# Feed-forward operands and the ring of split weights moved to addresses 64 bytes past a multiple of 128

## The chip, the cores and the metric

One core of one Trainium2 chip runs the whole kernel. The metric is the device time of one execution in microseconds (us), from three runs. The profile is one further execution on the same core; its rows count from that execution's first instruction.

## What is computed

One layer of a hybrid decoder on 512 prompt rows and 64 sample rows (576 columns in the kernel, which keeps everything transposed), width 1024:

```python
x = x + 0.5 * swiglu(rmsnorm(x, p['ffn1_norm']), p['ffn1_w_gate'], p['ffn1_w_up'], p['ffn1_w_down'])
h = rmsnorm(x, p['mix_norm'])
proj = h @ p['w_in']
...
x = x + jnp.concatenate([y_lru, y_pool], axis=-1) @ p['w_out']
x = x + cross_attend(rmsnorm(x, p['xattn_norm']), mem_k, mem_v, p['xattn_wq'], p['xattn_wo'])
x = x + 0.5 * swiglu(rmsnorm(x, p['ffn2_norm']), p['ffn2_w_gate'], p['ffn2_w_up'], p['ffn2_w_down'])
```

`swiglu(x, g, u, d)` is `(silu(x @ g) * (x @ u)) @ d` with an inner width of 2816. The two feed-forward steps are the first and the last of these lines.

## The kernel before

**Arithmetic.** Every large matrix product runs in float32r, split in two: a value is the sum of a rounded part (`h`, high) and the remainder (`l`, low), and a product is three matmuls: high by high, high by low, low by high (`mm3`, L159; `product`, L323). The stationary operand (128x128 weights, loaded by the PEld rows of the trace) is a weight block; the moving operand (288 columns, half of the 576) is a norm's output, a gated activation, or another activation.

**Stages.** Step f1 (`ffn`, L331, called at L688) runs from 0 to about 402 us, then the mixer's projections (`in_l`, `in_p`, `in_g`, then `wo`), the cross attention (`k`, `q`, `ss`, `s`, `v`, `sv`, `o`, `xo`), and from about 739 us step f2 (the same `ffn`, called at L1177) with the final norm in its last group.

**A step.** Of 22 chunks of 128 inner columns the first 3 (f1) or 2 (f2) are done with plain products (`std`, L351: two matmuls in a row with the same weights, one for each half of the columns). Each later chunk is done with seven products of twelve matmuls (`product`), on combinations of halves that `prepare_a` and `prepare_b` (L400, L412) make from the raw weights. From the fifth chunk on, the down projection of the group of chunks before (`down`, L448, names `pd`, `hh`, `hl`, `dh`, `dl`) is interleaved between the products by `fill` (L564); it too runs two matmuls per weight block. What is left of it runs alone after the last chunk: all of the last group in f1 (`down` with `after`, L629), in f2 as the tail with 320 and then 256 columns (L655 on). The order of TensorE's matmuls is fixed by a chain of dependencies in `mm` (L130).

**Where the operands lie.** Each SBUF partition is a byte range in which pools stack up from the left, or down from the right end (`side="right"`). Tiles are rounded to 32 bytes. The pools that matter, with the offset of their matmul operands from a multiple of 128 bytes as the built program places them:

| pool, tiles | what | offset |
|---|---|---|
| `wp`: `wr`, `wh`, `wl` (L71, L150, L348, L396) | raw weights and the ring of split weights; the stationary operand of all projections, and of the products but one | 96 |
| `s1`: `n1h`, `n1l` (L284, L679) | f1's normed input, moving | 96 |
| `f1`: `hh`, `hl`, `dh`, `dl`, `oh`, `ol` (L417, L442, L479) | f1's gated activations (moving) and down weights, and the seventh product's weights (stationary) | 64 |
| `s2`: `n2h`, `n2l` (L1154) | f2's normed input, moving | 64 |
| `f2`: as `f1` (L1177) | the same for f2 | 96 |
| `tail`: `th`, `tl` (L444) | down weights of f2's last group | 64 |
| `r1`, `r2`: `nm`, `y`, `nx`, `q` (L180) | moving operands of the projections between the steps | 96 |
| `xa`: `mh`, `ml`, `kk`, `pp` | operands of the cross attention | 64 |

All strides inside these tiles are multiples of 128 bytes (288 columns are 1152 bytes, a weight block's row 512), so a tile's offset holds for each of its slices. Below, a pair such as 96/64 is the offset of the moving operand over that of the stationary one.

Of the kernel before, what the change touches and what calls it, by code (L numbers as in the profile page):

```python
# [9 lines left out]
F32 = mybir.dt.float32  # L10
# [6 lines left out]
P = 128  # L17
# [48 lines left out]
def hybrid_step(ctx, tc, a):  # L66
# [3 lines left out]
    const = ctx.enter_context(tc.tile_pool(name="const", bufs=1))  # L70
    wp = ctx.enter_context(tc.tile_pool(name="wp", bufs=WSB))  # L71
    rows = ctx.enter_context(tc.tile_pool(name="rows", bufs=2))


    now, ends = {}, {}

    def begin(name, **kw):
        cm = tc.tile_pool(name=name, reuse_waits="tile", **{"bufs": 1, **kw})
        now[name] = cm.__enter__()
        ends[name] = cm  # L80
        return now[name]

    def end(*names):
        for name in names:
            ends.pop(name).__exit__(None, None, None)
            now.pop(name)
# [16 lines left out]
        return cst[:, c:c + 1]  # L103

    x = const.tile([P, DC, T], F32, name="x")
    ones = const.tile([P, 1], F32, name="ones")
    v.memset(ones, 1.0 / (DC * P))
    ident = const.tile([P, P], F32, name="ident")
# [32 lines left out]
    def split(hi, lo, src, scale=None):  # L141

        if scale is None:
            s.copy(hi, src)  # L144
            v.tensor_tensor(out=lo, in0=src, in1=f(hi), op=ALU.subtract)  # L145
        else:
            s.activation(hi, src, AF.Copy, scale=scale)
            v.scalar_tensor_tensor(out=lo, in0=src, scalar=scale, in1=f(hi), op0=ALU.mult, op1=ALU.subtract)
# [68 lines left out]
    def row_factor(accs, name, ps, n=T, parts=2):  # L217

        offs = blocks(n, parts)
        k = len(offs)
        ps = ps[:, 512 - k:512]
        u, y, q = (rows.tile([P, 8], F32, tag=f"rf{i}", bufs=1, name=f"rf{i}_{name}")[:, :k] for i in range(3))
        for i, o in enumerate(offs):
            for j, part in enumerate(accs):
                mm(ps[:, i:i + 1], lhsT=part[:, o:o + P], rhs=ones, start=j == 0, stop=j == len(accs) - 1)
        v.tensor_scalar(u, ps, EPS, None, op0=ALU.add)
        rsqrt(q, u, y)
        return q  # L230
# [92 lines left out]
    def product(out, w, n, b, start):  # L323

        for k in range(KP):
            for i, (qw, qx) in enumerate(((0, 0), (0, 1), (1, 0))):
                mm(out, lhsT=w(qw, k), rhs=n.part(qx, k, b), start=start and k == 0 and i == 0,
                   stop=k == KP - 1 and i == 2, skip_group_check=True)


    def ffn(name, n, fp, turn, plain, head=False):  # L331
# [240 lines left out]
        def finish_chunk(c):  # L572
            w, U, g, h_, l_ = c
            product(U, w["22"], n, T4, False)
            v.tensor_mul(g[:, :HT], U, g[:, :HT])
            split(h_, l_, g)

        for f in range(plain, FFC):
# [44 lines left out]
            fill()  # L623
            before = w, U, g, hh[gi][:, f - g0, :], hl[gi][:, f - g0, :]
        finish_chunk(before)
        after = turn()
        if after:
            down(gi, after)
# [11 lines left out]
        def finish(c0, c1, q, cuts):  # L640
            n2, h = c1 - c0, (c1 - c0) // 2
            pr = dual("rs")
            for i, o in enumerate(blocks(n2)):
                mm(pr[:, o // h, o % h:o % h + P], lhsT=q[:, i:i + 1].to_broadcast([P, P]), rhs=ident,
                   start=True, stop=True)
            for j0, j1 in zip(cuts, cuts[1:]):
                y = x[:, j0:j1, c0:c1]
                for i in range(2):
                    yh = y[:, :, i * h:(i + 1) * h]
                    v.tensor_mul(yh, yh, pr[:, i, :h].unsqueeze(1).to_broadcast([P, j1 - j0, h]))  # L650
                nc.sync.dma_start(a["o_y"][:, j0:j1, c0:c1], y)
# [23 lines left out]
            before_ = [acc[:, c0:c1], sq]  # L675
        finish(c0, c1, row_factor(before_, "f1", pd, c1 - c0), (0, 4, 6, 8))


    n1 = HalfNorm("g1", "n1", begin("s1", side="right"), acc=False)  # L679

    def to_mixer():
        nonlocal nm
        end("s1")
        nm = Norm("gm", "nm", begin("r1", side="right"))
        return nm.add

    nm = None
    ffn("f1", n1, begin("f1"), to_mixer, STD[0], head=True)  # L688
    end("f1", "ff")


# [3 lines left out]
    if True:  # L695
# [213 lines left out]
        for c in range(LC):  # L909
            gate_out(c)  # L910
    nc.sync.dma_start(a["o_small"], small)
    end("mix")


# [258 lines left out]
    def to_tail():  # L1173
        end("s2")
        begin("tail")

    ffn("f2", n2, begin("f2", side="right"), to_tail, STD[1])  # L1177
    end("f2", "tail", "ff")

# [110 lines left out]
```

## Time and profile before

| | |
|---|---|
| median of 3 runs | 1149.78 us (1148.24 to 1150.13) |
| profiled execution, its own time | 1148.76 us |
| its span, first to last instruction | 1146.7 us |
| TensorE matmul (PE) busy | 1129.4 us, 98% |
| weight loads (PEld) busy, beside the matmuls | 1113.0 us, 97% |
| VectorE (DVE) busy | 835.0 us, 73% |
| ScalarE (ACT) busy | 544.0 us, 47% |
| granted TensorE clock, mean | 0.997 |

Successive matmuls overlap in the trace: a row's duration (some 290 ns for 288 columns) is the way through the array, and the next one starts after some 132 ns. What a matmul costs is therefore the distance between starts, here called its pitch. It is read from the start times of a timeline, or as a window's length over the number of matmuls in it (a window counts up to three that only reach into it).

### The profile page before, as it was taken

Reading aid. Unit: us, or ns where it says so; the run is one execution under the profiler, and the core shown is the slowest. Engines: PE = TensorE matmul, PEld = TensorE weight load, DVE = VectorE, ACT = ScalarE, POOL = GpSimd, SP = SyncE. Lnnn points to the kernel's source line nnn. Section 1 sums busy time; section 2 is a strip of 40 time slices with the busy share of each in tenths; the row PEclk is TensorE's granted clock in tenths of the full one; section 3 lists DMA queues with packets and bytes.
Section 4 is the critical chain, followed back from the end, with each engine's and each line's share of the span. In section 5 each row is a group of like instructions: output and inputs, shape, how many; then the busy total and the mean of one; then the engine's idle time right before and its main releaser. Section 6 shows DMA issues by size and latency. Waiting matters only on the chain.

```text
span 1146.7 us, 20764 instructions
## 1 busy us (share of the span) xinstructions
PE 1129.4 (98%) x8634; PEld 1113.0 (97%) x8634; DVE 835.0 (73%) x1335; ACT 544.0 (47%) x852; POOL 24.1 (2%) x47
## 2 busy tenths in 40 slices
PE   8999999999999999999999999999999999999996
PEld 8999999999999999999998879999999999999996
DVE  8887787788774788977634566769877877877664
ACT  8644344444432555875622564545443443443343
POOL 0000000000000022110000000000000000000000
PEclk9999999999999999999999999999999999999998
DMA  8223233233221352232655753212333332332212
GB/s 294 94 83 110 75 93 101 83 95 115 80 81 51 116 177 60 71 128 87 224 199 181 281 201 93 74 37 84 93 93 91 94 92 75 106 104 72 88 47 83
DMA packets 44285, 126.30 MB, mean 110 GB/s; under 512 B 4832, under 2 KB 9952, under 8 KB 44064
## 3 DMA queue, kind: packets, MB, share of 16 engines
q1 hardware_dynamic: 41808, 122.84, 34.4%
q10 hardware_dynamic: 2384, 2.15, 0.6%
q8 instruction: 67, 1.10, 0.4%
q14 instruction: 26, 0.21, 0.1%
HBM read 120.16 MB, written 4.81 MB: 109 GB/s over the span
## 4 chain that ended last, share of the span: by engine, by line
PE 94%; DVE 3%; ACT 1%; issue 1%; DMA 0%; DVEq 0%
PE pd L132 25%; PE pu L132 23%; PE pc L132 11%; PE pa L132 5%; PE q L132 5%; PE wo L132 5%; PE xo L132 4%; PE pg L132 3%; PE k L132 2%; PE v L1024 2%; PE in_l L132 2%; PE in_p L132 2%; PE o L132 1%; PE s L132 1%; PE puc L132 1%; PE ss L992 1%
## 5 line engine op out<-in xcount | busy, mean ns | idle before, releaser
L132 PE MATMUL pd<-hh,dl 128*128 128x288 f32 (+2 forms) x644 | 139.6, 295 | 0.0
L132 PE MATMUL pd<-hh,dh 128*128 128x288 f32 (+2 forms) x644 | 139.1, 295 | 0.0
L132 PE MATMUL pd<-hl,dh 128*128 128x288 f32 (+2 forms) x644 | 138.9, 294 | 0.0
L132 PEld LDWEIGHTS pd<-hh,dh 128*128 128x128 f32 x644 | 103.9, 188 | 0.0
L132 PEld LDWEIGHTS pd<-hh,dl 128*128 128x128 f32 x644 | 103.5, 188 | 0.1
L132 PEld LDWEIGHTS pd<-hl,dh 128*128 128x128 f32 x644 | 103.2, 188 | 0.0
L144 ACT CAST oh_b<-r 128x512 fp32r<-128x512 f32 x39 | 24.2, 621 | 119.6 <-PE pa L132 107.1
L144 ACT CAST wh_e<-r 128x1024 fp32r<-128x1024 f32 x39 | 41.0, 1052 | 63.0 <-PE pu L132 56.9
L144 ACT CAST dh<-wr_d 128x512 fp32r<-128x512 f32 (+1 forms) x74 | 48.7, 658 | 40.8 <-PE pd L132 29.9
L464 DVE TENSOR_TENSOR x<-pd,x 128x576 f32<-128x576 f32 x72 | 54.3, 754 | 18.1 <-PE pd L132 18.1
L145 DVE TENSOR_TENSOR wl_e<-r,wh_e 128x1024 fp32r<-128x1024 f32 x39 | 47.7, 1223 | 13.2 <-ACT wh_e L144 13.2
L144 ACT CAST wh_g<-r 128x1024 fp32r<-128x1024 f32 x39 | 41.1, 1055 | 33.0 <-DVE r L420 29.2
L145 DVE TENSOR_TENSOR dl<-wr_d,dh 128x512 fp32r<-128x512 f32 (+1 forms) x74 | 54.0, 730 | 0.0
L145 DVE TENSOR_TENSOR wl_g<-r,wh_g 128x1024 fp32r<-128x1024 f32 x39 | 47.7, 1224 | 7.3 <-ACT wh_g L144 5.4
L145 DVE TENSOR_TENSOR wl_a<-r,wh_a 128x1024 fp32r<-128x1024 f32 x39 | 47.6, 1220 | 3.4 <-ACT wh_a L144 3.0
L603 DVE TENSOR_TENSOR g<-pc,u 128x288 f32<-128x288 f32 x39 | 17.8, 457 | 40.9 <-PE pc L132 40.6
L132 PE MATMUL pu<-n2h,wl_a 128*128 128x288 f32 x160 | 47.4, 296 | 0.0
L132 PE MATMUL pu<-n2h,wh_a 128*128 128x288 f32 x160 | 47.4, 296 | 0.0
L132 PE MATMUL pu<-n2l,wh_a 128*128 128x288 f32 x160 | 46.8, 293 | 0.5 <-DVE n2l L145 0.5
L610 DVE TENSOR_TENSOR g<-pa,rstd_n 128x288 f32<-128x288 f32 x39 | 17.8, 457 | 39.8 <-PE pa L132 39.4
L144 ACT CAST wh_a<-r 128x1024 fp32r<-128x1024 f32 x39 | 40.9, 1050 | 8.8 <-PE xo L132 3.5
L132 PE MATMUL pu<-n1l,wh_a 128*128 128x288 f32 x152 | 44.8, 295 | 0.0
(496 smaller groups left out, 3682.0 us busy)
## 6 DMA issues: line engine op xcount, KB each, us to landing
r<-f_gu SPq DMA_DIRECT2D x78, 512.0 KB, 3.7
wr_d<-f_d SPq DMA_DIRECT2D x48, 256.0 KB, 2.8
wr_d<-f_d SPq DMA_DIRECT2D x32, 320.0 KB, 3.1
ck<-ck SPq DMA_DIRECT2D x16, 512.0 KB, 4.6
cv<-cv SPq DMA_DIRECT2D x16, 512.0 KB, 7.1
wr_i<-w_in SPq DMA_DIRECT2D x12, 512.0 KB, 3.7
wr_s<-f_s SPq DMA_DIRECT2D x8, 512.0 KB, 4.6
wr_o<-w_out SPq DMA_DIRECT2D x8, 512.0 KB, 3.6
```

What stands on the lines that cost most here:

```text
L132: i = te.matmul(*args, **kw)
L144: s.copy(hi, src)
L145: v.tensor_tensor(out=lo, in0=src, in1=f(hi), op=ALU.subtract)
L464: v.tensor_add(halves(x[:, j, :]), pd[j][:, :, :HT], halves(x[:, j, :]))
L603: v.tensor_add(g[:, HT:], C, u2)
L610: v.tensor_mul(g[:, :HT], A, r[:, :HT])
L992: te.matmul(sps[b * 32:(b + 1) * 32, g, :ML], lhsT=z[:, 4 * g + b, j, :], rhs=t[:, b, :], start=j == 0, stop=j == DC - 1)
L1024: te.matmul(ps[:, m, :HD], lhsT=lhs[:, kd, ms], rhs=w[wi][:, k, :], start=kd == 0 and i == 0, stop=kd == DC - 1 and i == 2)
```

## The change

An unused tile of 8n float32, that is 32n bytes, is allocated in four pools. It shifts what follows it. The const pool lies at the left end, `wp` and `rows` behind it; `s1` and `f2` lie at the right end.

```diff
+    def odd(pool, n):
+
+        pool.tile([P, 8 * n], F32, bufs=1, name="odd")
...
     x = const.tile([P, DC, T], F32, name="x")
+    odd(const, 3)
     ones = const.tile([P, 1], F32, name="ones")
...
         finish_chunk(before)
+        if not head:
+            odd(fp, 1)
         after = turn()
...
         finish(c0, c1, row_factor(before_, "f1", pd, c1 - c0), (0, 4, 6, 8))
 
+    odd(rows, 1)
+
 
     n1 = HalfNorm("g1", "n1", begin("s1", side="right"), acc=False)
+    odd(now["s1"], 1)
```

(`fp` is the step's pool; `head` is true in f1 alone.) In the built program `wp` moves by 96 bytes, from offset 96 to 64; `n1h` and `n1l` from 96 to 64; all of `f2` from 96 to 64. What lay at 64 still does: `f1`'s and `s2`'s operands, the tail's and the attention's move by 128 or not at all. `r1` and `r2` stay at 96, since nothing is added in them. `ident` goes from 64 to 32, `ones` from 32 to 0. Every engine's instructions are the same as before in number, kind, shape, order and awaited semaphore counts; only addresses differ.

| matmuls of 288 columns | number | before | after |
|---|---|---|---|
| f1 plain products, and products from `wp` | 288 + 1368 | 96/96 | 64/64 |
| f1 products from `oh`, `ol` | 228 | 96/64 | 64/64 |
| f1 down projection | 1056 | 64/64 | 64/64 |
| f2 plain products, and products | 192 + 1680 | 64/96 | 64/64 |
| f2 down projection without the tail | 816 | 96/96 | 64/64 |
| `in`, `wo`, `q`, `xo` | 576 + 3 x 384 | 96/96 | 96/64 |

Of 256 columns, the 192 of `k` go from 64/96 to 64/64 and the 192 of `v` (weights moving) from 96/64 to 64/64; of the tail's 120 of 320 and 120 of 256 columns, 90 each go from 96/64 and 30 each from 96/96 to 64/64.

## Rows read from the trace of the kernel before

**Rows 1.** The page: busy time by engine, and the chain that ended last.
```profile
span 1146.7 us, 20764 instructions
...
PE 1129.4 (98%) x8634; PEld 1113.0 (97%) x8634; DVE 835.0 (73%) x1335; ACT 544.0 (47%) x852; POOL 24.1 (2%) x47
...
PE 94%; DVE 3%; ACT 1%; issue 1%; DMA 0%; DVEq 0%
```

**Rows 2.** Waits of PE alone: engine, line, releaser, us in total, times, longest.
```profile
PE pg L132 <- ACT wh L144: 5.5, 1, 5.5
PE rs L132 <- DVE rf_f L238: 1.4, 1, 1.4
PE pd L132 <- DVE x L661: 1.0, 2, 0.5
```

**Rows 3.** Timeline of PE: start, us, instruction; equal work of f1, first and last.
```profile
64.67 0.42 PE L132 MATMUL pd<-hh,dh 128*128 128x288 f32 x2
...
366.89 0.30 PE L132 MATMUL pu<-n1h,wl_a 128*128 128x288 f32 x1
```

**Rows 4.** The same view of f2, the same work.
```profile
795.34 0.42 PE L132 MATMUL pd<-hh,dh 128*128 128x288 f32 x2
...
1097.88 0.30 PE L132 MATMUL pu<-n2h,wl_a 128*128 128x288 f32 x1
```

**Rows 5.** Windows, tile pd alone: stretch, us, busy (count) by engine, clock, DMA.
```profile
64.60:366.80 302.20, 124.54 (x798) 111.58 (x798) 23.35 (x31) 0.00 (x0) 1.00 0.30 90
795.20:1097.70 302.50, 125.30 (x798) 112.26 (x798) 23.35 (x31) 0.00 (x0) 1.00 0.31 90
```

**Rows 6.** Windows, tile pa alone (product from `oh`, `ol`), the same stretches.
```profile
64.60:366.80 302.20, 31.61 (x216) 29.67 (x216) 8.24 (x18) 6.52 (x17) 1.00 0.30 90
795.20:1097.70 302.50, 31.42 (x216) 29.60 (x216) 8.24 (x18) 6.52 (x17) 1.00 0.31 90
```

**Rows 7.** Windows, PE: stretches of one kind of matmul without a stop.
```profile
368.00:400.00 32.00, 32.00 (x242) 1.00 0.33 95
495.00:525.00 30.00, 30.00 (x227) 1.00 0.42 135
705.00:735.00 30.00, 30.00 (x233) 1.00 0.29 88
743.00:751.00 8.00, 8.00 (x63) 1.00 0.01 2
```

**Rows 8.** Timeline of PE in f1's down projection alone, 64/64.
```profile
379.82 0.43 PE L132 MATMUL pd<-hh,dh 128*128 128x288 f32 x2
...
381.42 0.43 PE L132 MATMUL pd<-hh,dh 128*128 128x288 f32 x2
```

**Rows 9.** Timeline of PE in `wo`, 96/96.
```profile
495.88 0.43 PE L132 MATMUL wo<-yh,wl_o 128*128 128x288 f32 x2
...
496.69 0.42 PE L132 MATMUL wo<-yh,wl_o 128*128 128x288 f32 x2
```

**Rows 10.** Timeline of PE in `xo`, 96/96.
```profile
709.50 0.42 PE L132 MATMUL xo<-ql,wh_x 128*128 128x288 f32 x2
...
711.06 0.42 PE L132 MATMUL xo<-ql,wh_x 128*128 128x288 f32 x2
```

**Rows 11.** Timeline of PE in `k`, 256 columns, 64/96.
```profile
556.88 0.28 PE L132 MATMUL k<-mh,wh_k 128*128 128x256 f32 x1
...
557.60 0.28 PE L132 MATMUL k<-mh,wh_k 128*128 128x256 f32 x1
```

**Rows 12.** Timeline of PE in f2's tail, 256 columns, 96/64.
```profile
1125.18 0.28 PE L132 MATMUL pd<-hh,th 128*128 128x256 f32 x1
...
1126.23 0.28 PE L132 MATMUL pd<-hh,th 128*128 128x256 f32 x1
```

## The prediction, made before the changed kernel ran

> **What bounds the kernel now.** First the page: TensorE's matmuls are busy 98% of the span, and the chain that ended last lies 94% on PE [rows 1]. Then PE's waits: the longest is 5.5 us at the start, and the next two make 2.4 us together [rows 2]. There is no wait to win; the time is the sum of some 8,600 matmul pitches. What bounds the kernel is how closely matmuls follow each other, and an address can act there alone. VectorE (73%) and ScalarE (47%) [rows 1] could change their pace with an address too; it would be hidden under PE, which hardly ever waits for them.
>
> Then the pitch. At the granted clock of 1.00 [rows 7], its 2.4 GHz level, 288 columns would take 120.0 ns. The trace shows more. In f1's down projection alone, 12 matmuls take 381.42 - 379.82 = 1.60 us: 133.3 ns each [rows 8]. In `wo` 6 take 0.81 us, 135 ns at this resolution [rows 9]; over 30 us, 227 counted less the two that reach in from the side, 133.3 ns [rows 7]. In `xo` 12 take 1.56 us: 130.0 ns [rows 10]. So 10 to 13 ns lie on top of the columns, and they differ by place: 3.3 ns between `wo` and `xo`, which have the same shape, the same ring of weights and the same offsets, 96/96. Hence the offset alone doesn't set the pitch; there are patterns that TensorE falls into and keeps. At 256 columns, `k` (64/96) takes 0.72 us for 6, 120.0 ns [rows 11], the tail (96/64) 1.05 us for 9, 116.7 ns [rows 12]. That offsets play some part is likely; what part, these rows leave open.
>
> **A comparison that the trace holds.** f1 and f2 run the same 2286 matmuls from the first interleaved down projection to the last product: 798 of `pd` and 1488 of products. f1 takes 366.89 - 64.67 = 302.22 us [rows 3], f2 1097.88 - 795.34 = 302.54 us [rows 4]. In f1 the products are 96/96 (one in seven 96/64) and `pd` is 64/64; in f2 the products are 64/96 and `pd` is 96/96. The whole differs by 0.32 us, but its parts don't agree. `pd` at 64/64 is busy 124.54 us, at 96/96 125.30 us [rows 5]: 0.76 us / 798 = 0.95 ns less each. The products must then be 0.76 - 0.32 = 0.44 us cheaper in f2: 0.30 ns each in favour of 64/96. Of that the product from `oh` alone has (31.61 - 31.42) / 216 = 0.88 ns in favour of 64/96 against 96/64 [rows 6].
>
> **The change part by part.** It removes, adds and moves no instruction, no DMA and no wait; SP's and POOL's queues are the same. Only pitches can change.
>
> 1. f1's products, 96/96 to 64/64. No product stands at 64/64 before; the nearest row is `pd` at 64/64, interleaved with them, 0.95 ns cheaper than at 96/96 [rows 5]. 1368 x 0.95 = 1.30 us less, taken in full. Bounds: 3.3 ns less each if they fall into the pattern of `xo` [rows 10], 1 ns more if all of them run at 133.3 ns [rows 8] instead of the 132.2 ns that f1's loop has on average (302.22 / 2285, [rows 3]).
> 2. f1's 228 products from `oh`, 96/64 to 64/64: only the moving operand shifts. Half of the step, 0.1 us less; bounds as in 1.
> 3. f2's down projection, 96/96 to 64/64, 816 matmuls: 0.95 ns each, 0.78 us less. Before and after of this part both stand in the trace, so it is the surest.
> 4. f2's products, 64/96 to 64/64, 1680: they have 0.30 ns of the 0.95 already, so 0.65 ns each, 1.09 us less.
> 5. The plain products, 288 in f1 and 192 in f2, run by themselves. Alone, 64/64 has 133.3 ns [rows 8], 96/96 the same in `wo` [rows 7], and 64/96 some 131 to 133 (8.00 us over 60 or 61 of the 63 counted, the last line of [rows 7]): nothing.
> 6. The projections between the steps, 1728 matmuls, go from 96/96 to 96/64, by the ring alone. The two nearest rows contradict each other: in the loop 96/64 is dearer than 64/96 by 0.88 ns [rows 6], alone at 256 columns it is cheaper by 3.3 ns [rows 11, 12]. I take nothing. Upper end: `xo` loses its pattern, 231 matmuls in its 30 us of [rows 7], 3.3 ns each, 0.8 us more, and the others stay. Lower end: the other 1344 gain it, 4.4 us less.
> 7. `k`, `v` and the tail, between 116.7 and 120.0 ns a matmul on either side [rows 11, 12]: `k` may gain 192 x 3.3 ns = 0.6 us, the tail's 120 of 256 columns lose 0.4 us and its 120 of 320 as much, `v` lose 0.6 us. Between ends of either sign and of this size I take nothing.
>
> What hides the edits that I cost at nothing outside PE: casts and subtractions with other addresses, under PE's 98%; if one became slower, PE's waits would show it. Sum: 1.30 + 0.10 + 0.78 + 1.09 = 3.3 us less. Against the profiled execution's own 1148.76 us (span 1146.7 and 2.1 around it) that is 1145.5; that execution lies 1.0 us under the median of the runs, so against the median 1149.78 - 3.3 = **1146.5 us**, 0.29% less.
>
> **The rivals.**
>
> *Nothing changes* (1149.8 us). For it: alone, 64/64 and 96/96 both run at 133.3 ns [rows 7, 8]; the whole loop differs by 0.1% between two placements [rows 3, 4]. It may be that only the distance between the two operands counts, which is a multiple of 128 in both, and the 0.95 ns of `pd` come from its neighbours, the products. Against it: f2's products stand at a distance of 32 and change theirs to 0. The page "SBUF — State Buffer" of the Trainium skill, under Specifications, speaks for this rival: it gives cachelines of 16 bytes, of which 1152 contiguous bytes touch 72 from an offset of 64 as from 96. By that rule the term for `pd` would be zero, and so would the sum; the 0.76 us of rows 5 do not follow from it. "TensorE: Matmul & The Clock Gate", Part 2, adds that a weight load does not take read bandwidth from the running matmul, as it has a port of its own; no row here can show a port.
>
> *The projections fall into the pattern of `xo`* (1142.1 us). That pattern is in the trace, 130.0 ns over 30 us [rows 7]; with 96/64 the 256-column rows are at their quicker value too [rows 12]. The lower end of 6 comes on top of the forecast: 1146.5 - 4.4. Against it: every other stretch of 96/96 sits at 133.3.
>
> *The products lock at 133.3 ns* (slower, 1153.7 us). Alone, 64/64 runs at 133.3 ns over 32 us without a break [rows 7, 8], one of the dearest patterns of the trace. In the loops, products and `pd` now disturb each other with three different placements, and the average is 132.2. With one placement for everything the loops may settle in the pattern of f1's pure stretch: 3276 products x 0.95 ns = 3.1 us more, and `xo` loses 0.8. It decides from the point where the two loops' average, 132.3 ns now, passes 132.8: 2 x 2286 x 0.5 ns = 2.3 us more. Against it: f1's loop already has 64/64 `pd`, and there it is the cheaper one.
>
> That the change doesn't do what it says is excluded for the two steps by the built program's addresses; for the projections between them it is partly so, as `r1` and `r2` stay at 96.
>
> **How the numbers follow.** Forecast 0.45: own range 1145 to 1148.5. Nothing 0.21. The pattern of `xo` 0.16. Locked 0.18. About 0.2% (2.3 us) is what a measurement of this kernel can tell from no change, that is, under 1147.5 or over 1152.1. Of the forecast's case about 0.31 lies below, 0.14 within; the second is all within; the third all below; of the fourth 0.16 above and 0.02 within. Faster 0.47, same 0.37, slower 0.16. The range takes in the first two cases whole, half of the third and half of the fourth: 1142.5 to 1152.5.
>
> **What the changed profile would show.** Right: the same work of f1 takes 302.22 - 1.4 = about 300.8 us and that of f2 302.54 - 1.8 = 300.7 us, and f2's `pd` falls from 125.30 to about 124.5 us busy. `pd` of f1, unchanged in offset, keeps 124.5; if it moves by as much as the rest, neighbours and not offsets set the pitch. `wo` at 133.3 ns and `xo` at 130.0 keep theirs within 1 ns, or term 6 is wrong. Wrong as a whole: f1's loop at 302 or more, or a wait of PE over 1 us that isn't in rows 2.

## The result, and the profile after

The changed kernel takes 1153.12 us, the median of 8 runs (1151.30 to 1153.97), against 1149.74 us for the kernel before on the same chip. The ratio is 1.0027, with a 95% interval from 1.0018 to 1.0036: slower by 0.27%. The forecast was 1146.5 us, 0.29% faster, in a range up to 1152.5. Sign and range are both wrong. The profiled execution took 1153.97 us.

First the page of the kernel after, its span, PE and the chain's engines, beside [rows 1]:

```profile
span 1151.2 us, 20764 instructions
...
PE 1134.0 (99%) x8634; PEld 1117.7 (97%) x8634; DVE 834.6 (72%) x1335; ACT 543.1 (47%) x852; POOL 25.5 (2%) x47
...
PE 94%; DVE 3%; ACT 1%; issue 1%; DMA 0%; DVEq 0%
```

The span grew by 4.5 us and PE's busy time by 4.6, on as many instructions. Next PE's waits after, beside [rows 2] (engine and line, releaser, us in total, times, longest):

```profile
PE pg L137 <- ACT wh L149: 5.6, 1, 5.6
PE rs L137 <- DVE rf_f L243: 1.4, 1, 1.4
PE pd L137 <- DVE x L668: 1.0, 2, 0.5
```

No wait is new. As the prediction had it, only the pitch of matmuls can have moved. Then the equal work of the two loops, in the timeline of PE after (start, us, instruction), beside [rows 3, 4]:

```profile
64.92 0.43 PE L137 MATMUL pd<-hh,dh 128*128 128x288 f32 x2
...
368.56 0.30 PE L137 MATMUL pu<-n1h,wl_a 128*128 128x288 f32 x1
...
797.94 0.42 PE L137 MATMUL pd<-hh,dh 128*128 128x288 f32 x2
...
1100.71 0.29 PE L137 MATMUL pu<-n2h,wl_a 128*128 128x288 f32 x1
```

f1's loop takes 303.64 us where it took 302.22 (+1.42), f2's 302.77 where it took 302.54 (+0.23). Next the windows of `pd` alone after (stretch, us, busy and count of PE, PEld, DVE, ACT, clock, DMA share, GB/s), beside [rows 5]:

```profile
64.90:368.50 303.60, 125.65 (x798) 113.04 (x798) 23.37 (x31) 0.00 (x0) 1.00 0.31 90
797.00:1100.00 303.00, 124.74 (x798) 111.85 (x798) 23.34 (x31) 0.00 (x0) 1.00 0.31 90
```

`pd` of f2 fell from 125.30 to 124.74 us, as forecast. `pd` of f1, whose own offsets didn't change, rose from 124.54 to 125.65: the sign that the prediction had named for neighbours. Last the plain stretches, windows of PE after (stretch, us, busy and count, clock, DMA share, GB/s), beside [rows 7]:

```profile
368.00:400.00 32.00, 32.00 (x242) 1.00 0.31 89
495.00:525.00 30.00, 30.00 (x227) 1.00 0.41 135
705.00:735.00 30.00, 30.00 (x227) 1.00 0.31 95
```

f1's pure stretch and `wo` are as they were. `xo` went from 233 matmuls in 30 us to 227: from 130.0 to 133.3 ns each, +0.95 us over its stretch.

About 1.5 us of the span's 4.5 are not the change's. In the tail of this execution the granted clock fell to 0.50, the 1.2 GHz level, for some 3.4 us, in which 19 matmuls are counted instead of 32: 13 at some 117 ns are 1.5 us. Windows of PE after:

```profile
1124.00:1127.00 3.00, 2.48 (x22) 1.00 0.00 0
1127.70:1131.10 3.40, 3.40 (x19) 0.50 0.00 0
1131.20:1134.00 2.80, 2.80 (x26) 1.00 0.00 0
```

The same windows of the kernel before:

```profile
1124.00:1127.00 3.00, 3.00 (x27) 1.00 0.00 0
1127.70:1131.10 3.40, 3.40 (x32) 1.00 0.00 0
```

Shortly ahead of the fall PE had stood for 0.52 us and then run eight narrow matmuls for the final norm; so it does in the kernel before, whose clock stayed. Of the eleven profiles of the layer taken later, six show such a drop (3.4 us long, once 6.8) and five don't. A kernel that is faster than before (`d64`) is among the six, and the ring alone, as slow as the change, is among the five. So the drop doesn't go with the offsets.

### The profile page after: what moved, and what is told of

It reads as the page before. It is cut to its first block, busy times and chain, and to the rows that moved or that the text cites. A ratio compares the mean times of both kernels' runs of the same rounds, so it can differ in the third digit from the quotient of the medians.

```text
span 1151.2 us, 20764 instructions
## 1 busy us (share of the span) xinstructions
PE 1134.0 (99%) x8634; PEld 1117.7 (97%) x8634; DVE 834.6 (72%) x1335; ACT 543.1 (47%) x852; POOL 25.5 (2%) x47
## 4 chain that ended last, share of the span: by engine, by line
PE 94%; DVE 3%; ACT 1%; issue 1%; DMA 0%; DVEq 0%
PE pd L137 25%; PE pu L137 23%; PE pc L137 11%; PE pa L137 5%; PE q L137 5%; PE wo L137 4%; PE xo L137 4%; PE pg L137 3%; PE v L1034 2%; PE k L137 2%; PE in_l L137 2%; PE in_p L137 2%; PE o L137 1%; PE s L137 1%; PE puc L137 1%; PE ss L1002 1%
```

## The experiments

Below, the **distance** of a matmul is the offset of its stationary operand less that of its moving one, modulo 128 bytes: the table of the change lists 96/96 and 64/64 at distance 0, 64/96 at 32, 96/64 at 96. Pitches in the two tables of stages are means of the distances between starts, from the traces' start times, without the steps over 160 ns. Each ratio is against runs of the kernel before on the same chip (medians from 1149.62 to 1150.60 us), so a ratio, and not a time, is what compares one experiment with another.

**Two kernels that should change nothing.** `p256` adds an unused tile of 256 bytes, so every operand keeps its offset in 128; `w12` runs one warm-up matmul more.

```diff
+    const.tile([P, 64], F32, name="pad")
```
```diff
-WARM = 11
+WARM = 12
```

> The kernel before with one unused tile of 256 bytes in the const pool, so that everything in the left pools moves by 256 bytes and every operand keeps its offset from a multiple of 128 and of 256. If offsets set the pitch: 1149.7 us within 0.1%, the same stretches (f1's equal work 302.2 us, xo at 130.0 ns). If the pattern that TensorE falls into is a matter of chance that any change of the program draws anew: 1147 to 1154, with xo at 130.0 or 133.3 ns and f1's equal work between 302 and 304.

> The kernel before with 12 instead of 11 warm-up matmuls at the start, all addresses unchanged; the weights arrive later than the warm-up ends, so its work itself is hidden. If offsets set the pitch: 1149.7 us within 0.1% and xo at 130.0 ns. If the pattern depends on when the matmuls begin: 1147 to 1154, with xo or f1's loop changed by 1 us or more.

`p256`: 1150.24 us, ratio 1.0001 [0.9993, 1.0009]. `w12`: 1150.86, 1.0006 [0.9997, 1.0015]. f1's loop takes 302.35 us in both, as before, and `xo` 38.51 in both. The time of f1's loop is no matter of chance or of the exact address.

One stage did change in `p256`: `wo`, at the same offsets 96/96. Windows of PE, first of the kernel before, then of `p256`:

```profile
505.00:529.00 24.00, 24.00 (x182) 1.00 0.52 170
505.00:529.00 24.00, 24.00 (x187) 1.00 0.52 173
```

About a hundred matmuls into `wo` its pitch goes from 133.3 to 130.0 ns and stays there, which saves 0.6 us. `s1` below does the same; `w12`, `f2` and `rest`, with the same offsets in `wo`, don't. So one stage at one distance can run at either pitch.

**The ring alone.** The change without its pads in `s1` and `f2`.

```diff
     x = const.tile([P, DC, T], F32, name="x")
+    odd(const, 3)
...
+    odd(rows, 1)
```

> Only the ring of split weights moves to 64 (const and rows tiles of the change); n1 and all of f2 stay at 96. f1's products are then 96/64, f2's products 64/64, the projections 96/64, both down projections as before. If offsets set the pitch and the ring is what costs: xo at 133.3 ns (0.95 us more) and f1's equal work near 303.8 us, time near 1152. If n1's move to 64/64 costs in f1: f1's equal work stays at 302.2, time near 1150.7. If chance: no relation to the change's stretches.

1153.42 us, ratio 1.0029 [1.0020, 1.0039]: the whole slowdown. The loops in its timeline of PE:

```profile
64.79 0.43 PE L137 MATMUL pd<-hh,dh 128*128 128x288 f32 x2
...
367.91 0.30 PE L137 MATMUL pu<-n1h,wl_a 128*128 128x288 f32 x1
...
797.36 0.43 PE L137 MATMUL pd<-hh,dh 128*128 128x288 f32 x2
...
1100.77 0.29 PE L137 MATMUL pu<-n2h,wl_a 128*128 128x288 f32 x1
```

Both loops lose: 303.12 - 302.22 = +0.90 us and 303.41 - 302.54 = +0.87. `xo`, in the window of its 30 us, has the change's 133.3 ns:

```profile
706.00:736.00 30.00, 30.00 (x227) 1.00 0.30 88
```

**The other parts, alone and together.** `s1` moves n1's pool alone, `f2` the second step's pool alone, `rest` both, so it is the change with its ring undone (against the change):

```diff
     x = const.tile([P, DC, T], F32, name="x")
-    odd(const, 3)
...
-    odd(rows, 1)
```

> One part alone: only n1's pool is moved (n1 from 96 to 64), ring and f2's pool stay at 96. Step 1's products become 64/96, as step 2's were in the kernel before. Distance theory (the pitch goes by the stationary operand's offset less the moving one's, modulo 128; 32 is on the cheap side, 0 and 96 on the dear one): step 1's products fall from 132.51 to about 132.3 ns, that is 1488 x 0.2 = 0.3 us, pd unknown by up to 1 ns either way (0.8 us); stretches outside step 1, xo's 38.5 us among them, unchanged; time 1149.0, range 1148.2 to 1150.2, ratio 0.998 to 1.000. Rival, absolute offset (operands at 64 are cheap): only one operand of the products at 64, half of the forecast's term 1, about -0.65 us. Rival, the prediction's terms were right and only the ring's xo loss was missed: as the absolute one. No theory gives a slowdown; one would mean that pd's neighbours decide.

> One part alone: only the second step's pool is moved (its pd from 96/96 to 64/64, its oh to 64); products stay 64/96, the ring and n1 at 96. Distance theory: pd stays at distance 0, so step 2's loop changes only through pd's neighbours: within 0.5 us of 302.7 either way, time 1149.7 +- 0.6, ratio 0.9995 to 1.0005. Prediction's term 3 (64/64 is cheaper for pd): pd falls from 132.30 to 131.3 ns, -0.8 us, time 1149.0. Everything ahead of step 2 as before, xo's 38.5 us among them.

> The change without its ring: n1 and f2's pool are moved to 64, the ring of split weights stays at 96. Theory R (the ring alone makes the loss: it puts the loops' products at distances that their cycle pays for, and takes xo out of its 130.0 ns state): the two parts, each without effect alone, stay without effect together, 1149.9 +- 0.8, ratio 0.9993 to 1.0008, xo 38.5 us, step 1's loop 302.3 and step 2's 302.5. Rival, parts that only act together (n1 and f2 at 64 cost time whatever the ring): step 1's loop unchanged, since f2's pool stands behind it, so the rival would have to act in step 2's and reach 303 us.

1150.05 us, 1.0002 [0.9993, 1.0011]; 1150.48, 1.0005 [0.9996, 1.0014]; 1150.02, 0.9997 [0.9986, 1.0007]: nothing, alone or together. `s1` took f1's products from distance 0 to 32, and their pitch stayed (132.51 and 132.53 ns), where the distance theory wanted 0.2 ns less. `f2` took `pd` from 96/96 to 64/64 and got 0.06 ns of the prediction's 0.95 (132.30 to 132.24): inside its bursts the steps fell from 132.37 to 131.88 ns, but the step from a burst to the next product rose from 131.91 to 134.26 and took it back.

**Streams of matmuls by themselves.** `micro` computes no layer: it runs, for each of 16 pairs of offsets, 96 matmuls of 288 columns as pairs (two halves on the same weights), then 96 singles.

```diff
+    for rep in range(REPS):
+        for om, ow in PLACES[rep]:
...
+                            mm(pair[:, h, :HT], lhsT=w[:, ow + k * P:ow + k * P + P],
+                               rhs=x[:, om + k * T + h * HT:om + k * T + h * HT + HT],
```

> Nothing of the layer is computed: TensorE runs 96 matmuls of 288 columns in pairs with the same weights, then 96 singly, for each of 16 placements (moving and stationary operand at 0, 32, 64, 96 bytes past a multiple of 128), twice; the second time each placement begins after three fp32 matmuls of one column. No other engine works beside it. If offsets set the pitch: each placement has one pitch, the same in both passes, and 64/64 differs from 96/96 and 96/64 by 0.3 ns or more. If only the distance counts: 0/0, 32/32, 64/64 and 96/96 agree within 0.2 ns. If patterns are entered by chance: the same placement gives 130 in one pass and 133 in the other.

From its timeline of PE, the first matmul of five successive stretches and one further on: moving at 0, stationary at 64 (pairs, singles), stationary at 96 (pairs, singles); then 32/32 (pairs, and the first of its singles).

```profile
72.51 0.43 PE L94 MATMUL pair<-mh,wh 128*128 128x288 f32 x2
...
85.20 0.29 PE L94 MATMUL one<-mh,wh 128*128 128x288 f32 x1
...
97.90 0.43 PE L94 MATMUL pair<-mh,wh 128*128 128x288 f32 x2
...
110.70 0.29 PE L94 MATMUL one<-mh,wh 128*128 128x288 f32 x1
...
123.60 0.43 PE L94 MATMUL pair<-mh,wh 128*128 128x288 f32 x2
...
149.19 0.42 PE L94 MATMUL pair<-mh,wh 128*128 128x288 f32 x2
...
162.00 0.29 PE L94 MATMUL one<-mh,wh 128*128 128x288 f32 x1
```

At distance 64, 96 matmuls take 12.69 us (132.2 ns each) as pairs and 12.70 as singles; at 96, 12.80 (133.3) and 12.90 (134.4); at 32/32, 12.81 as pairs. Over all 16 places the steady pitch goes by the distance, whatever the offsets themselves: pairs 132.2 at 64 and 133.3 at 0, 32 and 96; singles 132.2 at 32 and 64, 133.3 at 0, and 133.3 or 134.4 at 96. These are streams of one kind of matmul, and no place gave 130.0 here.

**Where 130.0 comes from.** `micro2` repeats such stretches, 48 matmuls each, behind one matmul of 8 to 296 columns.

```diff
+        for n in SLIPS:
+            mm(stop[:, :n], lhsT=wh[:, :P], rhs=mh[:, :n], start=True, stop=True)
```

> Only streams of matmuls, no layer is computed. Moving operand at 96, stationary at 64 past, 96, 0 and 32 in turn with the distance 0, 32, 64 and 96; ahead of each stretch of 48 stands one matmul of another width (8 to 296 columns), which shifts the phase between the stream and its weight loads. Distance theory in its plain form: each stretch settles at the pitch of its distance (pairs 132.2 at 64, 133.3 else; singles 132.2 at 32 and 64, 133.3 at 0 and 96) whatever the slip. Theory of several steady states: some slips leave a stretch at 130.0 ns, as xo showed, and only at some distances (0 among them, 96 not, by what the runs so far show of xo). Chance: pitches that differ between equal slips with no order in distance.

Four of these short matmuls in its timeline, ahead of pairs at distance 0, 96/96:

```profile
45.42 0.18 PE L91 MATMUL stop<-mh,wh 128*128 128x48 f32 x1
...
51.78 0.19 PE L91 MATMUL stop<-mh,wh 128*128 128x64 f32 x1
...
58.27 0.21 PE L91 MATMUL stop<-mh,wh 128*128 128x96 f32 x1
...
64.78 0.22 PE L91 MATMUL stop<-mh,wh 128*128 128x128 f32 x1
```

With its short matmul the stretch takes 6.36 us behind 48 columns, 6.49 and 6.51 behind 64 and 96: at distance 0 a stream of pairs has two steady pitches, 130.0 and about 133.3 ns, and its start decides which. Behind 16 to 48 and 280 columns it was 130.0, behind the others not (the stretch behind 8 columns began before the clock had risen). At distances 32, 64 and 96, and for singles, none of the 13 starts led to 130.0. But singles at distance 96 (96/64) settled at 134.4 ns behind 200 and 280 columns and at 133.3 behind the rest, so the 134.4 of `micro` need not belong to its one place.

`slip` tries it in the kernel before, at its own offsets: one extra matmul of 32 columns, overwritten at once, ahead of each chunk of `in`, `q` and the first halves of `wo`, and once in f1's pure stretch.

```diff
+    def jolt(ps, w, xx, k):
+        mm(ps[:, 0, :32], lhsT=w[0][:, k, :], rhs=xx[0][:, k, :32], start=True, stop=True)
...
+        if slip:
+            jolt(ps, w, xx, order[0])
```

> The kernel before, all offsets unchanged, and one extra matmul of 32 columns (its result is overwritten) ahead of the first matmul of each chunk of in, wo (first halves) and q, and once ahead of step 1's pure stretch. Theory S (at distance 0 a stream of pairs has two steady states, 133.3 and 130.0 ns, and a short matmul ahead of it puts it into the second): the stretches behind a slip run at 130.0 until something interrupts them; step 1's pure stretch 34.40 to about 33.7 us, q -0.4, in -0.6, wo -0.3, each slip itself paid with 0.11 us; time 1148.0, range 1147.0 to 1149.3. Rival, xo's 130.0 has another cause than a state entered at its start (its data, its queue, the place in the program): all stretches stay at 133.3 and the 30 slips cost 1 to 3 us: 1151 to 1153.

1152.82 us, ratio 1.0021 [1.0012, 1.0030]: a miss. In the timeline some chunks do change over:

```profile
420.70 0.43 PE L132 MATMUL in_l<-nml,wh_i 128*128 128x288 f32 x2
...
423.37 0.43 PE L132 MATMUL in_l<-nmh,wl_i 128*128 128x288 f32 x2
...
424.01 0.42 PE L132 MATMUL in_p<-nml,wh_i 128*128 128x288 f32 x2
...
426.35 0.42 PE L132 MATMUL in_p<-nml,wh_i 128*128 128x288 f32 x2
```

20 matmuls ahead of a slip take 2.67 us (133.5 ns), 18 behind it 2.34 us (130.0). But most of `q` and f1's pure stretch stayed at 133.3, and `xo`, to which nothing was done, lost its 130.0:

```profile
705.00:735.00 30.00, 30.00 (x227) 1.00 0.32 95
```

So `xo`'s pattern hangs on how the stream comes in, as well as on the distance.

**The loops' cycle by itself.** `micro3` runs 12 products as singles and 6 `pd` as pairs in turn, for 64 sets of distances, then three sets behind slips.

```diff
+    for ow in OFF:
+        for ou in OFF:
+            for od in OFF:
+                cycles(0, ow, ou, od, 10)
```

> Only streams of matmuls, no layer is computed: the loops' cycle of 12 products and 6 pd, ten times over for each of the 64 sets of distances (moving operand of the products at 0; their weights, pd's moving operand and pd's weights each at 0, 32, 64, 96), then three sets (all at 64 as in the change; step 1's of before; all at distance 64) behind slips of 13 widths. Theory of cycles (the mean of a cycle is set by the distances within the products, within pd and across their borders): sums of a cycle order as the loops did: all at 64 apart 2378 ns, step 1 of before 2381, ring at 64 with n at 96 2388, all together at one offset 2385 to 2392 and more than one value for it, by the slip. Rival (the loops' pitches came from other traffic, not from the addresses): all sets within 2 ns of one another.

A cycle of 18 takes from 2373 to 2407 ns by the set, so addresses alone do spread it by 1.4%. But the order is not that of the loops: all operands at one offset is among the cheap ones here (2376 ns) and the dear one in the change, and one and the same set (all 64 apart) settles at 2373 or at 2380 by the slip ahead, and at 2393 with all offsets 32 further on. So where kinds of matmul alternate, the distances alone don't give the time, even without the layer. This stream doesn't stand for the loops.

**The ring at the other two offsets, and everything 64 apart.** `r32` and `r0` place the ring alone at 32 and at 0. `d64` places ring, down weights, `oh` and `th` at 32 and all moving operands at 96; `d64s` is `d64` with all of them 32 bytes further on, so that the ring stands at 64 as in the change. The core of `d64` (`r32` and `r0` are as the ring alone, with 2 and 2, or 1 and 3, in place of 3 and 1; `d64s` has 3 in the const pool and 3 in a pool ahead of `s1`):

```diff
     x = const.tile([P, DC, T], F32, name="x")
+    pad(const, 2)
...
+        pad(fp, 2)
...
+        if not head:
+            pad(fp, 2, "pad2")
...
+        pad(tp, 2)
...
+    pad(rows, 3)
```

> All operands placed so that moving and stationary stand 64 apart: ring at 32, n1, n2, r1, r2 and hh at 96, dh and oh at 32, tail's th at 32. Distance theory: the plain stretches fall from 133.3 to 132.2 ns (f1's pure 258 matmuls, in 687, part of wo 376, q 449: about 1770 x 1.1 = -1.9 us), xo, which stood at 130.0, rises to 132.2 (288 x 2.2 = +0.6 us) as does k's and v's mix by at most 0.2; the loops' products and pd stay near 132.2, -0.3 to -1.5 us for both together. Time about 1147.8, range 1146.5 to 1149.5, ratio 0.997 to 1.000. Absolute-offset theory (64 is the cheap place): nothing stands at 64 here, so no gain: 1149.8 or, with xo's pattern lost, 1150.7. If the plain stretches stay at 133.3, the distance theory falls outside the stream measurement.

> The ring of split weights alone, at 32 in place of 96; everything else as before. Distance theory (stationary less moving, modulo 128; products in the loops at 64 about 132.2 ns, at 32 132.3 to 132.5, at 0 132.5 to 132.9, at 96 133.1): step 1's products (96/32, distance 64) fall to 132.2 ns, step 2's (64/32, distance 96) rise to 133.1; the plain stretches (96/32, distance 64) fall to 132.2 and in, wo and q as they did with all at 64 apart (91.35, 49.9, 59.5 us); xo 39.1 us. Time: -0.5 + 1.1 - 1.0 + 0.6, about 1149.9, range 1148.8 to 1151. Rival (any move of the ring away from where it stood costs, by slots and not by distance): both loops slower, in, wo and q unchanged, 1152 or more.

> The ring alone, at 0. Distance theory: step 1's products (96/0, distance 32) 132.3 to 132.5 ns, step 2's (64/0, distance 64) 132.2, so neither loop is slower; plain stretches (96/0, distance 32) stay at 133.3; xo, away from distance 0, loses its 130.0 ns: 38.5 to about 39.4 us. Time +0.9 - 0.3, about 1150.3, range 1149.3 to 1151.2. Rival (slots, not distance): both loops slower as with the ring at 64, 1152 or more.

> All operands 64 apart as in the run d64, and every one of them 32 bytes further on: ring, dh, oh and th at 64, where the change has them, and n1, n2, r1, r2, hh and xa's at 0. Distance theory: nothing but the differences counts, so the stage times are those of d64 (step 1's loop 301.98, step 2's 302.12, in 91.35, q 59.5, xo 39.1 us) and the time is 1147.3 +- 0.8, ratio 0.997 to 0.9985. Rival, the ring's place at 64 is in itself the dear one (absolute offset): loops at 303 and the time at 1151 or more.

`d64` 1147.31 us, ratio 0.9977 [0.9969, 0.9986]; `r32` 1151.03, 1.0007 [0.9999, 1.0016]; `r0` 1150.31, 1.0004 [0.9995, 1.0012]; `d64s` 1147.76, 0.9976 [0.9967, 0.9984]. The page of `d64s`, and its windows of PE:

```profile
span 1146.5 us, 20764 instructions
```
```profile
368.00:400.00 32.00, 32.00 (x244) 1.00 0.35 98
495.00:525.00 30.00, 30.00 (x230) 1.00 0.41 135
705.00:735.00 30.00, 30.00 (x229) 1.00 0.27 83
```

Two matmuls more fit into f1's 32 us and three into `wo`'s 30; `xo`, at 229, has neither 130.0 nor 133.3. (The span holds a drop of the clock in the tail, as in the profile after.) With the ring at 64 as in the change, the kernel is the faster one. The place itself is innocent; what it is paired with decides. Stages, us (a loop up to the first matmul behind it, `xo`'s last 288 matmuls with eight of f2 behind them, `q` with the score matmuls among it), and the pitch of `pd` in the loops, ns; below it the products. The distance there is that of six products of seven, those from the ring; the seventh, from `oh`, has the same only in `after`, `d64`, `d64s`, before's f2 and ring's f1:

| | before | ring | r32 | r0 | after | d64 | d64s |
|---|---|---|---|---|---|---|---|
| f1 loop | 302.35 | 303.25 | 302.63 | 302.42 | 303.77 | 301.98 | 302.10 |
| f2 loop | 302.67 | 303.54 | 303.75 | 302.81 | 302.90 | 302.12 | 302.65 |
| `in`, `wo` and `q` | 201.71 | 201.95 | 200.78 | 201.92 | 201.88 | 200.75 | 200.68 |
| `k` | 23.89 | 23.69 | 23.56 | 23.45 | 23.69 | 23.02 | 23.14 |
| `xo` | 38.51 | 39.46 | 39.13 | 39.45 | 39.46 | 39.13 | 39.15 |
| f1 `pd`, distance 0 (64 in d64, d64s) | 131.75 | 131.71 | 132.16 | 131.88 | 133.01 | 131.84 | 131.83 |
| f2 `pd`, the same | 132.30 | 132.68 | 132.47 | 132.48 | 131.63 | 131.84 | 132.10 |

| products, by distance | pitch in ns, kernel and step |
|---|---|
| 64 | 132.21 and 132.22 (d64), 132.33 and 132.42 (d64s), 132.34 (r0, f2), 132.50 (r32, f1) |
| 32 | 132.34 (before, f2), 132.26 (`f2`, f2), 132.49 (r0, f1), 132.53 (`s1`, f1) |
| 0 | 132.51 (before, f1), 132.73 (ring, f2), 132.82 and 132.90 (after) |
| 96 | 133.02 (r32, f2), 133.15 (ring, f1) |

The forecasts for the plain stretches and `xo` came out: `r32`'s `in`, `wo` and `q` are those of `d64`, `r0`'s `xo` lost its 130.0. Of the loops, `r32` put f2's products to 96 and paid 0.7 ns on each (132.34 to 133.02), as forecast, but f1's at 64 gained nothing (132.50 where 132.2 was forecast). Of `d64`'s gain 1.0 us lies in `in`, `wo` and `q`, 0.9 in the two loops and 0.9 in `k`, of which the last was not forecast; `xo` gave back 0.6.

## Why the prediction was wrong

**What held.** The bound: nothing but pitches moved, and no wait appeared [rows 1, 2]. Term 5, the plain products, was small, as taken: f2's 192 took 28.10 us for 28.28, and f1's 288, which begin at the lower clock, 45.00 for 44.77. Term 7 was small too: `k` gained 0.2 us, `v` lost about as much, the tail's 320 columns kept their pitch.

**The step that failed** is the price of terms 1 to 4: "1368 x 0.95 = 1.30 us less", taken from `pd` at 64/64 against 96/96 [rows 5], and used as the worth of the offset 64. The 0.95 ns was no property of `pd`'s offset, and it was read too large. Busy time takes in two long steps at the start of f2's loop, where two pairs take 0.33 and 0.38 us in place of 0.26 (timeline of PE before):

```profile
795.60 0.43 PE L132 MATMUL pd<-hl,dh 128*128 128x288 f32 x2
795.93 0.54 PE L132 MATMUL pd<-hh,dl 128*128 128x288 f32 x2
796.31 0.30 PE L132 MATMUL pu<-n2h,wh_e 128*128 128x288 f32 x1
```

It also leaves out the step from a burst of `pd` to the next product, which is shorter in f2. From the starts, `pd` had 131.75 ns in f1 and 132.30 in f2, 0.54 apart, and the products 132.51 and 132.34, 0.17 apart in place of 0.30. Nor is the smaller figure the offset's: between f1 and f2 the products beside `pd` differ too, and when the change left f1's `pd` where it was and moved those, its busy time rose by 1.11 us / 798 = 1.4 ns. Conversely `f2` alone changed the offset and its `pd` gained 0.06. Term 3's size nearly came (125.30 to 124.74, 0.56 us of 0.78), but only beside products that had become dearer.

By term: 1 and 2 together were to bring -1.4 us, and f1's loop came to +1.42: 0.31 ns on 1488 products make 0.46 us, 1.26 ns on 798 unchanged `pd` make 1.0. Terms 3 and 4 were to bring -1.8 us in f2's loop, by the check that the prediction set, and it came to +0.23: its products, which term 4 had at 0.65 ns less, went from distance 32 to 0 and from 132.34 to 132.90 ns (+0.8 us), `pd` gave back 0.67 ns each (-0.5).

**Term 6 was taken at zero and was its upper bound.** `xo` left distance 0 for 96 and lost its 130.0 ns: 0.95 us against the 0.8 stated there. The lower end, -4.4 us, doesn't exist: 96/64 led to 130.0 nowhere.

**The sum.** f1's loop 1.42, f2's 0.23 and `xo` 0.95 make 2.6 us; with small differences of other stages it is about 3.0 of the span without the drop of the clock, and the medians differ by 3.4.

**The rivals.** "Products lock at 133.3 ns, and `xo` loses 0.8" gave 1153.7 us and is the nearest, in part by luck: the products cost 1.3 us of its 3.1, and 1.0 us came from f1's `pd`, which it left alone. The average of the two loops did not reach its point of 132.8 ns (303.64 us / 2285 = 132.9 in f1, 132.5 in f2), and it wasn't a lock of the products: their bursts still spread from 132.5 to 133.5 ns. Its reason, one placement for everything, is not the cause, as the ring alone costs as much with placements still mixed. "Nothing changes" named a half of the cause, that distance counts rather than offset; that f2's products go from 32 to 0 was noted there against it, and term 4 gave that step the wrong sign. From the 16-byte cachelines of the page "SBUF — State Buffer" of the Trainium skill, Specifications, the prediction had worked out an estimate of zero; the ring's +0.29% disagrees with it.

**What is shown, and what stays open.** Shown: the ring's move alone makes the loss; n1's and f2's make none; the same ring at 64 is harmless when the moving operands stand 64 away, although `ones` and `ident` are shifted there as in the change; streams of one kind outside the layer follow the distance, within the two steady states that some distances have. Not settled is the loops' own pitch. After the change f1 and f2 have the same offsets throughout, yet `pd` takes 133.01 ns in the one and 131.63 in the other (inside its bursts some 134.0 in 79 of f1's 120, some 131.5 in 91 of f2's), and `d64s` repeats `d64`'s distances with 0.5 us more in f2's loop. Distance orders the products (64 and 32 below 0, 0 below 96) only to within 0.3 ns. That several steady patterns exist and that the entry picks one is shown for pairs at distance 0 and for singles at 96; that this is what parts f1 and f2 is only argued. Whether the traffic of the other engines and of the DMAs, which the streams lack, takes part in the loops' pitch was not tested.

## What to carry to other kernels

When float32r matmuls of this width run back to back with a weight load for each, try placing the moving and the stationary operands 64 bytes apart modulo 128; here that gave 0.23% with no other edit, and the dear choice cost 0.29%. An address's price is read from a pair of operands and their neighbours: before one row's difference is carried over to other matmuls, ask what else differs between the two rows. And move one operand at a time, since here two parts did nothing and the third did it all. And before an average difference of busy time is used as a pitch, look for single long steps in it.

## What the runs showed of the hardware that was not expected

- With a weight load for each matmul of 288 columns, the steady pitch of a stream of one kind (`micro`, `micro2`) took one of four values: 130.0, 132.2, 133.3 and 134.4 ns. In `micro` the distance modulo 128 of the two operands decided, not the offsets themselves, but for the singles of one place of 16 (moving 0, stationary 96: 134.4 where the others of its distance had 133.3). In the mixed cycle of `micro3` it did not: one set of distances gave 2373, 2380 and 2393 ns.
- At distance 0, pairs on the same weights have two steady states, 130.0 and 133.3 ns. One matmul of 16 to 48 columns at the start puts the stream into the faster one. In the layer `wo` changed over at unchanged offsets modulo 128 (`p256`), and `xo` lost the faster state without an edit of its own (`slip`). Singles at distance 96 have two as well, 133.3 and 134.4.
- The granted clock fell to 0.50 for 3.4 us (once 6.8) in the tail in seven of the thirteen profiles of the layer, behind a stop of 0.5 us and eight narrow matmuls that all of them have; in the profile after that was 1.5 us, nearly half of what this change does.
